# Key and query copies on ScalarE, constants and first weights at other places

## The chip, the cores and the metric

The kernel runs on one core of one Trainium2 chip. Its time is the device time of one execution in microseconds (us). The engines are named as the profile names them: PE (TensorE), ACT (ScalarE), DVE (VectorE), POOL (GpSimd) and SP (SyncE, which issues most of the DMA transfers). Each engine works through its own queue of instructions in order, and waits on semaphores for what the others must have done.

## The reference

A decoder trunk of two layers on one sequence of 512 tokens of width 1024, in float32. A layer is

```python
f = _swiglu(_rmsnorm(h, ffn1_pre_g[l]), ffn1_w_gate[l], ffn1_w_up[l], ffn1_w_down[l])
h = h + 0.5 * _rmsnorm(f, ffn1_post_g[l])
```

then a mixing step, then a second half-step of the first form. The mixing step projects the normalized h to queries, keys and values and adds three branches, each through its own output matrix and a sigmoid gate, before a common matrix `w_out`:

- stick-breaking attention, 8 heads of 64 channels, where the weight of a key is a sigmoid times the products of what later keys leave over;
- forgetting attention ("fox"), 8 heads of 64, a softmax whose logits get `c[q] - c[k]`, with `c` the running sum of the logarithms of forget gates;
- attention to a memory of 256 rows, 4 heads of 128.

## The kernel before

All matrix products are done in three passes. `split` writes a float32 value as a rounded high part (ACT, line 189 or 192) and the rest as a low part (DVE, line 190 or 193), and `mm3` adds high by high, high by low and low by high (lines 203 to 205). So each weight block of 128x1024 costs ACT one cast (`wh_...`), DVE one subtraction (`wl_...`) and PE its matmuls. Names are made of a letter for the tile, the layer, and numbers; the profile leaves the numbers out.

A layer runs as four stages: network a (gate and up products, tiles `pta`, in groups of hidden blocks `TG`, then down products), mixing (projections, heads, branch products `pb`), the product with `w_out` (`pwo`), and network c (`ptc`). The gate and up products go by a scheme of sums of weight blocks (`kta`, `ktc`) and of input blocks (`aga`, `ra`).

Heads go in pairs. A key projection `pk` (128 rows, 64 for each head) is split by halves into `k`: the high part of head j stands in `k[r, j]` with its own 64 rows `r`, and the other 64 rows `ro` of that tile are filled with a copy (lines 1544 and 1546), since the matmul contracts over 128 rows, high and low queries stacked. For the stick heads (branch 0) the low part is copied as well, in one instruction on two planes. The scores are `zs` (line 1317) or `zf` (1359 to 1367). A fox head adds a second matmul on `qk` (1367), a tile that `fox_pre` puts together from a copy of the queries, a copy of the low keys (1347, 1348), ones, and the running sums `cs` times a selector. `forget_cumsum` makes `cs`, with two copies (1462). The probabilities are then transposed and split (`pts`, `ptf`), multiplied with the values (`pvs`, `pvf`) and summed and split to `o`.

The PSUM bank of `pk` is read by ACT (high) and by DVE (low), and the build puts each reader of one tile behind the last one where they are on different engines.

What is issued when: the kernel text writes its work through a job queue `Q`. A job has weight units that are loaded ahead and a generator of products; `Q.add` appends, `Q.weave` and `Q.spawn` put generators with waits between the products, and `Q.past(mark, us)` holds a head until so much product time lies behind its projection (`W_K` is 4.0). `down` is used for the down products and for `w_out` alike: its job `first` loads the second half's weights, and with them the first two units of the next network (`marks["next"][0]`); its job `second` loads the first half's weights again, one unit behind each step. After that the build sorts the instructions of every engine by its own planning, so the place in the text is a wish and not the place in the queue. The places named below are those of the built queues.

Of the kernel before, what the change touches and what calls it, by code (L numbers as in the profile page):

```python
# [9 lines left out]
F32 = mybir.dt.float32  # L10
# [12 lines left out]
def kernel(  # L23
# [47 lines left out]
    NH = 8  # L71
# [637 lines left out]
    def ffn(l, src, wg, wu, wd, dst, name, spare, aside=None):  # L709
# [335 lines left out]
        if name == "a0":  # L1045
            Q.add([], vectors)
            Q.add([], lambda: iter(mem_squares() or ()))
        for g in TG[1:]:
            todo = after if g == TG[1] and after is not None else turns(g)
            some(1 if todo is after else 2)  # L1050
            over, later[:] = later[1:], later[:1]
            behind()
            some(7)
            later[:] = over
# [24 lines left out]
    def down(w, ktiles, act, emit, name, dst, marks, before=None, carry=False):  # L1079

        PAIRS = ((0, 1), (2, 3))
        AFTER = {(0, 0): ((0, 1),), (0, 1): ((1, 1),), (1, 1): ((2, 1), (3, 1)), (2, 1): ((2, 0),), (2, 0): ((3, 0),)}
        banks = {}

        def seed(hf, ts):

            for t, b in AFTER.get((ts[0], hf), ()) if carry else ():
                parts = HALVES if halves(b, t) else (FULL,)
                banks[t, b] = [pbank("mm", f"p{name}_{b}_{t}_{i}") for i in range(len(parts))]
                for pt, c in zip(banks[t, b], parts):
                    nc.scalar.activation(pt[:, c], dst.fs[t][:, HF[b]][:, c], AF.Copy, scale=-1.0 if b else 1.0)

        def halves(hf, t):
            return t == NT - 1 and dst.g_pre is None and hf == 0  # L1100

        def tiles(uns, hf, ts, done=None):
            seeded = (ts[0], hf) in banks
            pts = [banks.pop((t, hf))[0] if seeded else pbank("mm", f"p{name}_{hf}_{t}") for t in ts]
            for un in uns:
                for k in range(un.nk):
                    kk = un.k0 + k
                    for t, pt in zip(ts, pts):
                        ah, al = act(kk, slice(t * P, (t + 1) * P))
                        mm3(pt[:], ah, al, un.h[:, k], un.l[:, k], kk == 0 and not seeded, kk == ktiles - 1, seeded)  # L1110
                        yield 3 * S * PE_US
                    if kk == 1:
                        seed(hf, ts)
                if done is not None:
                    done()
            for t, src in [(t, emit(t, hf, pt[:], seeded)) for t, pt in zip(ts, pts)]:
                dst.result(t, hf, src)

        def at_last(uns, hf, t):

            parts = [(c, pt) for c, pt in zip(HALVES, banks.pop((t, hf)))]
            for i, (c, pt) in enumerate(parts):
                for un in uns:
                    for k in range(un.nk):
                        kk = un.k0 + k
                        ah, al = act(kk, slice(t * P, (t + 1) * P))
                        mm3(pt[:, c], ah, al, un.h[:, k, c], un.l[:, k, c], False, kk == ktiles - 1, True)
                        yield 3 * S // 2 * PE_US
                dst.last_part(t, hf, c, pt[:, c], i)

        def late(uns, hf, t):
            if halves(hf, t):
                yield from at_last(uns, hf, t)
                return
            Q.hold = True
            ends = t == NT - 1 and not marks["next"][0]
            yield from tiles(uns, hf, (t,), (lambda: Q.load_next(1)) if ends else None)
            Q.spawn(dst.chain(t))
            if ends:
                Q.hold = False  # L1140

        uns = [[Unit(w, k, 2, hf * S, S, f"{name}_{i}_{k}") for k in range(0, ktiles, 2)] for i, hf in enumerate((0, 1, 0))]

        def first():
            for un in uns[1] + marks["next"][0]:
                un.load()
            if before is not None:
                before()
            dst.gains()
            yield from tiles(uns[0], 0, PAIRS[0])  # L1150

        def second():

            again = iter(uns[2])
            yield from tiles(uns[1], 1, PAIRS[1], lambda: next(again).load())

        Q.add(uns[0], first)
        marks["next"] = [], []
        marks["late"] = Q.add([], lambda: iter(()))
        for t in PAIRS[0]:  # L1160
            Q.add(uns[1] if t == 0 else [], lambda t=t: late(uns[1], 1, t))
        Q.add(marks["next"][0], second)
        for t in PAIRS[1]:
            marks["end"] = Q.add(uns[2] if t == 2 else marks["next"][1], lambda t=t: late(uns[2], 0, t))

# [176 lines left out]
    def fox_pre(q, k, j, hd, cs, name):  # L1342

        r, ro, _ = HEAD_ROWS[j]
        rs_ = slice(ro.start, min(ro.stop, 104))
        qk = stile([P, 2, S], "rs", "qk" + name)
        nc.gpsimd.tensor_copy(qk[r, 0], q[r, j])
        nc.gpsimd.tensor_copy(qk[r, 1], k[r, 2])
        nc.gpsimd.memset(qk[ro, 0].bitcast(F32), 1.0)
        nc.vector.tensor_scalar(qk[rs_, 1], cs[rs_].bitcast(F32), sel[rs_, hd:hd + 1], None, ALU.mult)  # L1350
        return qk
# [89 lines left out]
    def forget_cumsum(l, fl, holder):  # L1441

        pt = pbank("mm", f"pfl{l}")
        for t in range(NT):
            nc.tensor.transpose(pt[:NH, t * P:(t + 1) * P], fl[:, t], ident[:])
        yield 0.3
        a, b = tmp(f"fa{l}")[:NH], tmp(f"fb{l}")[:NH]  # L1450

        nc.scalar.activation(a, pt[:NH], AF.Abs, bias=bfor[:, l:l + 1])
        nc.scalar.activation(a, a, AF.Exp, scale=-1.0)
        nc.scalar.activation(a, a, AF.Ln, bias=one_t[:NH])
        nc.vector.scalar_tensor_tensor(a, pt[:NH], nbfor[:, l:l + 1], a, ALU.min, ALU.subtract)
        nc.vector.tensor_tensor_scan(b, bfor[:, l:l + 1].broadcast_to([NH, S]), a, 0.0, ALU.add, ALU.add)
        cs = stile([P, S], "cs", f"cs{l}")
        nc.gpsimd.memset(cs[:].bitcast(F32), 0.0)
        nc.scalar.copy(cs[0:NH], b)
        nc.vector.tensor_tensor(cs[32:32 + NH], b, cs[0:NH].bitcast(F32), ALU.subtract)  # L1460
        for c in (0, 32):
            nc.gpsimd.tensor_copy(cs[64 + c:64 + c + NH], cs[c:c + NH])
        holder["cs"] = cs

    def mixing(l, src, ks, vs, values, dst):
# [62 lines left out]
        def proj(key, un, scale):  # L1528
            nm = f"{key[0]}{l}_{key[1]}_{key[2]}"
            pt = pbank("mm", "p" + nm)  # L1530
            yield from gemm(pt[:], [un], 0, act)
            if key[0] == "q":

                t = st[key] = blk("q", nm)
                for r, ro, j in HEAD_ROWS:
                    split(t[r, j], t[ro, j], pt[r], scale=scale)
            else:

                twice = key[1] == 0
                t = st[key] = stile([P, 4 if twice else 3, S], "k", nm)  # L1540
                for r, ro, j in HEAD_ROWS:
                    split(t[r, j], t[r, 2 + j if twice else 2], pt[r])
                    if twice:
                        nc.gpsimd.tensor_copy(t[ro, j::2], t[r, j::2])
                    else:
                        nc.gpsimd.tensor_copy(t[ro, j], t[r, j])

        def project_v(br, p):

# [206 lines left out]
        def run():  # L1756
# [47 lines left out]
            def causal(n):  # L1804

                if n % 2 == 0:
                    Q.past(marks[heads[n // 2]], W_K, Q.limit)
                if n == NH:
                    Q.until(marks["mem"])
                    st["o", 1] = [blk("o", f"o{l}_1_{p}") for p in range(NP)]  # L1810
# [123 lines left out]
    for l in LAYERS:  # L1934
        i, mn = 3 * l, []
        ma = ffn(l, subs[i], ffn1_w_gate, ffn1_w_up, ffn1_w_down, subs[i + 1], f"a{l}", "v",
                 lambda l=l, mn=mn: mem_norm(l, mn))
        values = mem_kv(l, mn, *kvs[l])
        mb = mixing(l, subs[i + 1], *kvs[l], values, subs[i + 2])
        if l == 0:  # L1940
            Q.weave(begin(), ma["first"])
            more_constants()
        else:
            for part, units in zip(mc["next"], (ma["early"][:2], ma["early"][2:])):
                part.extend(units)
            boundary(mc, mc["end"], ma["first"])
        boundary(ma, ma["end"], mb["first"])
        mb["run"]()
        mc = ffn(l, subs[i + 2], ffn2_w_gate, ffn2_w_up, ffn2_w_down, subs[i + 3], f"c{l}", "o")
        for part, units in zip(mb["next"], (mc["early"][:2], mc["early"][2:])):  # L1950
                part.extend(units)
        boundary(mb, mb["end"], mc["first"])
# [25 lines left out]
```

## Time and profile before

| what | value |
|---|---|
| median of 3 runs | 2342.62 us (2340.15 to 2343.8) |
| the profiled execution: its own time, its span | 2341.6 us, 2339.8 us |
| PE busy | 2326.2 us, 99% |
| DVE busy | 1815.4 us, 78% |
| ACT busy | 1429.4 us, 61% |
| POOL busy | 246.6 us, 11%, 330 instructions |
| granted clock | 0.999 |

A time such as 811.07 is counted from the start of the span. The second layer's mixing runs as the first one's, some 1158 us later. A row of a timeline has start, duration, engine, line, operation and shapes, and in brackets how long the engine stood idle before it and what ended that.

### The profile page before, as it was taken

Reading aid. Unit: us, or ns where it says so; the run is one execution under the profiler, and the core shown is the slowest. Engines: PE = TensorE matmul, PEld = TensorE weight load, DVE = VectorE, ACT = ScalarE, POOL = GpSimd, SP = SyncE. Lnnn points to the kernel's source line nnn. Section 1 sums busy time; section 2 is a strip of 40 time slices with the busy share of each in tenths; the row PEclk is TensorE's granted clock in tenths of the full one; section 3 lists DMA queues with packets and bytes.
Section 4 is the critical chain, followed back from the end, with each engine's and each line's share of the span. In section 5 each row is a group of like instructions: output and inputs, shape, how many; then the busy total and the mean of one; then the engine's idle time right before and its main releaser. Section 6 shows DMA issues by size and latency. Waiting matters only on the chain.

```text
span 2339.8 us, 32552 instructions
## 1 busy us (share of the span) xinstructions
PE 2326.2 (99%) x12232; PEld 1994.8 (85%) x12232; DVE 1815.4 (78%) x2407; ACT 1429.4 (61%) x2307; POOL 246.6 (11%) x330
## 2 busy tenths in 40 slices
PE   9999999999999999999999999999999999999998
PEld 8888889998888888888888888889988888888887
DVE  8766978676898887769887679786768988866696
ACT  6655766665665465567665567656656655556574
POOL 1101100100122011101011110011001210111110
PEclk9999999999999999999999999999999999999999
DMA  8866858753232676669586767587423326776682
GB/s 247 236 174 181 228 179 249 199 163 108 73 110 72 234 218 182 167 167 256 171 217 170 185 190 228 190 238 227 135 76 91 100 83 232 219 189 169 180 224 99
DMA packets 241697, 412.74 MB, mean 176 GB/s; under 512 B 12650, under 2 KB 78466, under 8 KB 241028
## 3 DMA queue, kind: packets, MB, share of 16 engines
q1 hardware_dynamic: 200992, 326.74, 42.5%
q0 software_dynamic: 37088, 71.34, 17.7%
q10 hardware_dynamic: 3460, 12.59, 1.4%
q8 instruction: 96, 1.57, 0.3%
q14 instruction: 61, 0.50, 0.1%
HBM read 383.35 MB, written 27.26 MB: 175 GB/s over the span
## 4 chain that ended last, share of the span: by engine, by line
PE 90%; DVE 5%; DMA 3%; ACT 1%; issue 1%; SPq 0%; POOL 0%; DVEq 0%; ACTq 0%; POOLq 0%
PE ptc L203 5%; PE ptc L205 5%; PE ptc L204 5%; PE pta L203 5%; PE pta L205 5%; PE pta L204 5%; PE g L203 3%; PE g L204 3%; PE g L205 3%; PE pdc L203 3%; PE pda L205 3%; PE pdc L205 3%; PE pdc L204 3%; PE pda L204 3%; PE pda L203 3%; PE pv L203 1%
## 5 line engine op out<-in xcount | busy, mean ns | idle before, releaser
L190 DVE TENSOR_TENSOR wl_tc<-ktc,wh_tc 128x1024 fp32r<-128x1024 f32 x80 | 97.7, 1223 | 63.3 <-ACT wh_tc L189 63.3
L190 DVE TENSOR_TENSOR wl_ta<-kta,wh_ta 128x1024 fp32r<-128x1024 f32 x80 | 97.6, 1223 | 57.8 <-ACT wh_ta L189 57.8
L205 PE MATMUL pta<-wh_ta,aga 128*128 128x512 f32 x320 | 124.7, 390 | 1.3 <-DVE aga L190 1.3
L189 ACT CAST wh_tc<-ktc 128x1024 fp32r<-128x1024 f32 x80 | 84.1, 1054 | 67.9 <-PE ptc L205 48.0
L203 PE MATMUL pta<-wh_ta,aga 128*128 128x512 f32 x320 | 125.2, 392 | 0.0
L203 PE MATMUL ptc<-wh_tc,agc 128*128 128x512 f32 x320 | 125.1, 393 | 0.0
L205 PE MATMUL ptc<-wh_tc,agc 128*128 128x512 f32 x320 | 124.6, 389 | 0.0
L204 PE MATMUL ptc<-wl_tc,agc 128*128 128x512 f32 x320 | 124.6, 389 | 0.0
L204 PE MATMUL pta<-wl_ta,aga 128*128 128x512 f32 x320 | 124.6, 389 | 0.0
L189 ACT CAST wh_ta<-kta 128x1024 fp32r<-128x1024 f32 x80 | 84.1, 1053 | 65.7 <-PE pta L205 41.8
L190 DVE TENSOR_TENSOR wl_tc<-raw_tc,wh_tc 128x1024 fp32r<-128x1024 f32 x56 | 68.6, 1224 | 45.4 <-ACT wh_tc L189 45.3
L190 DVE TENSOR_TENSOR wl_ta<-raw_ta,wh_ta 128x1024 fp32r<-128x1024 f32 x58 | 70.9, 1224 | 41.9 <-ACT wh_ta L189 41.8
L189 ACT CAST wh_ta<-raw_ta 128x1024 fp32r<-128x1024 f32 x58 | 60.9, 1052 | 45.5 <-PE pta L205 38.0
L189 ACT CAST wh_tc<-raw_tc 128x1024 fp32r<-128x1024 f32 x56 | 59.0, 1054 | 47.8 <-PE ptc L205 36.6
L203 PE MATMUL ptc<-wh_tc,us_b 128*128 128x512 f32 x224 | 87.7, 391 | 0.2
L203 PE MATMUL pda<-wh_da,aa 128*128 128x512 f32 x224 | 87.5, 391 | 0.0
L203 PE MATMUL pdc<-wh_dc,ac 128*128 128x512 f32 x224 | 87.5, 391 | 0.0
L205 PE MATMUL ptc<-wh_tc,us_b 128*128 128x512 f32 x224 | 87.2, 389 | 0.0
L204 PE MATMUL ptc<-wl_tc,us_b 128*128 128x512 f32 x224 | 87.2, 389 | 0.0
L205 PE MATMUL pda<-wh_da,aa 128*128 128x512 f32 x224 | 87.2, 389 | 0.0
L204 PE MATMUL pda<-wl_da,aa 128*128 128x512 f32 x224 | 87.2, 389 | 0.0
L204 PE MATMUL pdc<-wl_dc,ac 128*128 128x512 f32 x224 | 87.2, 389 | 0.0
(593 smaller groups left out, 7932.7 us busy)
## 6 DMA issues: line engine op xcount, KB each, us to landing
raw_ta<-in_ffn_w_gate_dram SPq DMA_DIRECT2D x44, 512.0 KB, 4.4
raw_tc<-in_ffn_w_gate_dram SPq DMA_DIRECT2D x44, 512.0 KB, 4.7
raw_da<-in_ffn_w_down_dram SPq DMA_DIRECT2D x42, 512.0 KB, 3.8
raw_dc<-in_ffn_w_down_dram SPq DMA_DIRECT2D x42, 512.0 KB, 3.6
kta<-in_ffn_w_up_dram SPq DMA_DIRECT2D x40, 512.0 KB, 6.2
raw_wg<-in_w_gate_dram SPq DMA_DIRECT2D x40, 512.0 KB, 4.7
ktc<-in_ffn_w_up_dram SPq DMA_DIRECT2D x40, 512.0 KB, 5.7
kt<-in_w_gate_dram SPq DMA_DIRECT2D x24, 512.0 KB, 5.9
```

The source lines that it names most:

```text
L189: both = [nc.scalar.copy(h_ap, src)]
L190: make = lambda: nc.vector.tensor_tensor(l_ap, src, h_ap.bitcast(F32), ALU.subtract)
L203: nc.tensor.matmul(pt, lh, rh, start=start, stop=False, skip_group_check=free)
L204: nc.tensor.matmul(pt, lh, rl, start=False, stop=False, skip_group_check=free)
L205: nc.tensor.matmul(pt, ll, rh, start=False, stop=stop, skip_group_check=free)
```

## The change

1. The copies of keys, queries and `cs` that POOL made are made by ACT. The copy of the keys' high part reads the PSUM bank `pk` in place of the tile `k`, and the one instruction for high and low planes of a stick head becomes two.
2. `more_constants`, which was called before everything else of layer 0 but the start, becomes a job ahead of the third group of hidden blocks of the first network.
3. In `down` without `carry` (that is, in the product with `w_out`) the first units of the next network are loaded in `second`, behind its third and fourth unit, and not in `first`.
4. `W_K` is raised by 1.5 for the first fox head. The built queues are the same on all engines with and without this edit.

```diff
+            if g == TG[2] and name == "a0":
+                Q.add([], lambda: iter(more_constants() or ()))
...
         def first():
-            for un in uns[1] + marks["next"][0]:
+            for un in uns[1] + (marks["next"][0] if carry else []):
                 un.load()
...
             again = iter(uns[2])
-            yield from tiles(uns[1], 1, PAIRS[1], lambda: next(again).load())
+            ahead = itertools.chain((None, None), () if carry else marks["next"][0], itertools.repeat(None))
+
+            def load():
+                for un in (next(again), next(ahead)):
+                    if un is not None:
+                        un.load()
+
+            yield from tiles(uns[1], 1, PAIRS[1], load)
...
-        Q.add(marks["next"][0], second)
+        Q.add(marks["next"][0] if carry else [], second)
...
-        nc.gpsimd.tensor_copy(qk[r, 0], q[r, j])
-        nc.gpsimd.tensor_copy(qk[r, 1], k[r, 2])
+        nc.scalar.copy(qk[r, 0], q[r, j].bitcast(F32))
+        nc.scalar.copy(qk[r, 1], k[r, 2].bitcast(F32))
...
-            nc.gpsimd.tensor_copy(cs[64 + c:64 + c + NH], cs[c:c + NH])
+            nc.scalar.copy(cs[64 + c:64 + c + NH], cs[c:c + NH].bitcast(F32))
...
                     split(t[r, j], t[r, 2 + j if twice else 2], pt[r])
+                    nc.scalar.copy(t[ro, j], pt[r])
                     if twice:
-                        nc.gpsimd.tensor_copy(t[ro, j::2], t[r, j::2])
-                    else:
-                        nc.gpsimd.tensor_copy(t[ro, j], t[r, j])
+                        nc.scalar.copy(t[ro, 2 + j], t[r, 2 + j].bitcast(F32))
...
-                    Q.past(marks[heads[n // 2]], W_K, Q.limit)
+                    Q.past(marks[heads[n // 2]], W_K + (1.5 if n == NH else 0.0), Q.limit)
...
-            more_constants()
```

The lines move: in the changed kernel the key copies are 1552 and 1554, `qk` 1356 and 1357, `cs` 1471, `zs` 1326, `zf<-qk` 1376.

ACT at the product with `w_out` of layer 0, first two tiles, before (`wh_wo` is the high part of a block of `w_out`, `w_tc` of the next network's first weights, `sqb` sums squares of `pwo`):

```order
L189 CAST wh_wo_1_4_7834<-raw_wo_1_4_7776 128x1024
L623 ACTIVATE sqb_0_0_7930,nfb_0_7872<-pwo_0_0_7880 128x512
L189 CAST w_tc_0_0_0_7846<-raw_tc_0_0_0_7826 128x1024
L189 CAST wh_wo_1_6_7840<-raw_wo_1_6_7816 128x1024
L189 CAST w_tc_0_0_2_7851<-raw_tc_0_0_2_7832 128x1024
L623 ACTIVATE sqb_1_0_7933,nfb_1_7873<-pwo_0_1_7881 128x512
```

and where the `w_tc` rows stand in the changed kernel, one stage later (`us_b` is the next network's input):

```order
L189 CAST wh_wo_2_6_7952<-raw_wo_2_6_7852 128x1024
L623 ACTIVATE sqb_3_1_8119,nfb_3_7873<-pwo_1_3_8022 128x512
L189 CAST w_tc_0_0_0_8078<-raw_tc_0_0_0_7950 128x1024
L192 ACTIVATE us_b_0_8089<-utb_1_0_8132 128x4x128
L189 CAST w_tc_0_0_2_8111<-raw_tc_0_0_2_7956 128x1024
L192 ACTIVATE us_b_1_8090<-utb_1_1_8139 128x4x128
```

The two casts left the first pass over `w_out` and stand among those of the second token tile's input; `wh_wo_1_6` follows `sqb` directly now.

ACT at the third stick pair (`k_0_2`), before:

```order
L189 CAST k_0_2_5749<-pk_0_2_5676 64x512
L189 CAST o_0_1_4615<-ss_1_0_5735 64x512
L189 CAST k_0_2_5749<-pk_0_2_5676 64x512
L189 CAST pts_1_1_5795<-pts_1_1_0_5797 128x512
L189 CAST pts_1_1_5795<-pts_1_1_1_5804 128x384
L189 CAST pts_1_1_5795<-pts_1_1_2_5810 128x256
```

and in the changed kernel:

```order
L189 CAST k_0_2_5753<-pk_0_2_5680 64x512
L189 CAST o_0_1_4615<-ss_1_0_5739 64x512
L1552 CAST k_0_2_5753<-pk_0_2_5680 64x512
L1554 CAST k_0_2_5753<-k_0_2_5753 64x512
L189 CAST k_0_2_5753<-pk_0_2_5680 64x512
L189 CAST pts_1_1_5801<-pts_1_1_0_5803 128x512
L1552 CAST k_0_2_5753<-pk_0_2_5680 64x512
L1554 CAST k_0_2_5753<-k_0_2_5753 64x512
L189 CAST pts_1_1_5801<-pts_1_1_1_5810 128x384
L189 CAST wh_v_1_2_3_5768<-raw_v_1_2_3_5618 128x792
L189 CAST pts_1_1_5801<-pts_1_1_2_5816 128x256
```

Four copies stand between the casts, two of them ahead of the second cast of `pts`, and the cast of a value weight has come ahead of the third. PE's queue at this place has changed too: `zs_2_0`, `pvs_1_1` and the first rows of `pq_0_3`, which stood one behind the other, are interleaved.

ACT at the first fox heads, from the weight cast on, before:

```order
L192 ACTIVATE wh_wb_0_0_0_6440<-raw_wb_0_0_0_6273 128x1024
L189 CAST k_1_2_6433<-pk_1_2_6384 64x512 x2
L189 CAST wh_q_1_0_6541<-raw_q_1_0_6382 128x1024
L1371 ACTIVATE pf_2_0_3_6497,stf_2_0_6485<-zf_2_0_3_6489,stf_2_0_6485 128x512
L1371 ACTIVATE pf_2_0_2_6504,stf_2_0_6485<-zf_2_0_2_6488,stf_2_0_6485 128x384
```

and in the changed kernel:

```order
L192 ACTIVATE wh_wb_0_0_0_6448<-raw_wb_0_0_0_6281 128x1024
L189 CAST k_1_2_6441<-pk_1_2_6392 64x512
L1552 CAST k_1_2_6441<-pk_1_2_6392 64x512
L189 CAST k_1_2_6441<-pk_1_2_6392 64x512
L1357 CAST qk_2_0_6488<-k_1_2_6441 64x512
L1552 CAST k_1_2_6441<-pk_1_2_6392 64x512
L1357 CAST qk_2_1_6530<-k_1_2_6441 64x512
L189 CAST wh_q_1_0_6549<-raw_q_1_0_6390 128x1024
```

Four copies that were POOL's stand in ACT's queue here, and four more (two of `cs`, two of `qk` from the queries) ahead of the weight cast.

## The prediction

> **What bounds the kernel now.** I read the page first: the busy shares, then the chain that ended last.
>
> ```profile
> PE 2326.2 (99%) x12232; PEld 1994.8 (85%) x12232; DVE 1815.4 (78%) x2407; ACT 1429.4 (61%) x2307; POOL 246.6 (11%) x330
> PE 90%; DVE 5%; DMA 3%; ACT 1%; issue 1%; SPq 0%; POOL 0%; DVEq 0%; ACTq 0%; POOLq 0%
> ```
>
> TensorE (PE) works 99% of the span and POOL is 0% of the chain. The change removes no matmul, so all it can win is idle time of PE. The waits of PE say how much there is (us in total, times, longest):
>
> ```profile
> PE pwo L204 <- DVE wl_wo L190: 1.6, 2, 0.9
> PE zf L1367 <- POOL qk L1348: 1.4, 2, 1.0
> PE pta L205 <- DVE aga L190: 1.3, 1, 1.3
> PE zf L1359 <- DVE ptf L190: 0.5, 2, 0.2
> ```
>
> These are the waits that the change can touch: 4.8 us. Read by start to start (a 512-column fp32r matmul follows the last one after 0.23 us, see the two `pwo` rows below) each costs a little more, because PE starts late and its pipeline has run empty. So the ceiling of any gain is near 5.5 us, 0.23% of 2341.6. Below I call a difference under 0.2% (4.7 us) no change; that is about what a measurement of this kernel can tell. What remains is what the change adds to ScalarE (ACT), a queue served in order, and whether PE waits for that.
>
> **Part 1, w_out: the next network's first weights move away.**
>
> ```profile
> 807.56 1.05 ACT L189 CAST w_tc<-raw_tc 128x1024 fp32r<-128x1024 f32 x1 [1.78 <-DMA raw_tc<-in_ffn_w_gate_dram]
> 808.52 1.04 ACT L189 CAST wh_wo<-raw_wo 128x1024 fp32r<-128x1024 f32 x1
> 809.79 1.22 DVE L190 TENSOR_TENSOR wl_wo<-raw_wo,wh_wo 128x1024 fp32r<-128x1024 f32 x1
> 809.68 0.44 PE L203 MATMUL pwo<-wh_wo,ms 128*128 128x512 f32 x1
> 811.07 0.50 PE L204 MATMUL pwo<-wl_wo,ms 128*128 128x512 f32 x1 [0.95 <-DVE wl_wo L190]
> ```
>
> ACT stands 1.78 us at `w_tc` for a transfer; `wh_wo` is queued behind it, `wl_wo` behind that on VectorE (DVE), and PE starts 1.39 us after the row before instead of 0.23: 1.16 us lost. In layer 1 the same wait is shorter (1.6 in total less 0.95 is 0.66), about 0.82 start to start. With the two `w_tc` rows gone, ACT is free some 1.5 us earlier and DVE has 1.2 us less ahead, so both waits go: **−2.0 us**. Both ends: 0 if `raw_wo` itself lands late, −2.0.
>
> Where they go: their two transfers are issued behind the save of h, their casts stand between those of the second tile's `us_b`.
>
> ```profile
> raw_tc<-in_ffn_w_gate_dram SPq DMA_DIRECT2D x6, 512.0 KB, 4.2
> 834.64 1.28 DVE L193 SCALAR_TENSOR_TENSOR us_b<-utb,us_b 128x512 fp32r<-128x512 f32 x2
> 841.30 0.39 PE L203 MATMUL ptc<-w_tc,us_b 128*128 128x512 f32 x1
> ```
>
> On DVE two 1.2 us subtractions come ahead of `us_b`, which moves its end from 835.92 to about 838.8 with the wait for ACT; PE wants it at 841.3 less the 1.2 us won, 840.1. So 1.3 us of cover are left, against a landing of 4.2 us after issue. I take 0; gone, it costs what the transfer is later than 1.3 us.
>
> **Part 2, start: the constants go behind the second group.** On DVE they stand between 28.5 and 35.8, on POOL two selections are among them.
>
> ```profile
> 28.51 0.17 DVE L144 MEMSET c<- 128x128 f32 x1
> ...
> 35.63 0.17 DVE L159 COPY sel<-c 104x8 f32<-104x8 f32 x1
> ...
> 44.81 1.06 ACT L1174 ACTIVATE mst<-mst 128x1024 f32<-128x1024 f32 x1 [3.99 <-DMA mst<-in_mem_dram]
> 59.48 2.35 DVE L190 TENSOR_TENSOR aga<-ra,aga 128x1024 fp32r<-128x1024 f32 x2
> 59.05 0.39 PE L204 MATMUL pta<-wl_ta,aga 128*128 128x512 f32 x1
> 60.76 0.50 PE L205 MATMUL pta<-wh_ta,aga 128*128 128x512 f32 x1 [1.31 <-DVE aga L190]
> 69.93 1.23 DVE L190 TENSOR_TENSOR wl_ta<-raw_ta,wh_ta 128x1024 fp32r<-128x1024 f32 x1
> 121.87 1.22 DVE L190 TENSOR_TENSOR wl_ta<-kta,wh_ta 128x1024 fp32r<-128x1024 f32 x1
> ```
>
> The constants' time on DVE, by their rows some 2.6 us, does not come out at the other end: ACT still waits for `mst` until 44.81, and `hida` and `aga_3` hang behind it. What is won is one 1.1 us row (a `kta` subtraction) that now runs in DVE's idle time before 46, so `aga` begins at 58.4 and PE waits 0.4 instead of 1.5: −1.1. But the new order has PE take four instead of two matmuls of the group's `wh_ta_4_0_0` early, and DVE has four small `mem_rstd` rows and one `wl_ta` more before its `wl_ta_4_0_0` (69.93 before, about 71.6 now) where PE arrives at about 70.8: +0.8. Net **−0.3 us**, between −1.5 and +0.8. At their new place they stand around the `wl_ta` at 121.87, which PE takes up at about 130, so some 7 us cover their 2.6: nothing.
>
> **Part 3, the copies.** All of POOL's copies go to ACT, which has 98 instructions more, 49 a layer. Two of POOL's groups:
>
> ```profile
> L1544 POOL CAST k<-k 64x1024 fp32r<-64x1024 f32 x16 | 17.3, 1080 | 80.1 <-DVE k L190 49.0 <-issue 31.1
> L1348 POOL CAST qk<-k 64x512 fp32r<-64x512 f32 x16 | 11.9, 743 | 11.4 <-DVE k L190 11.0
> 672.15 0.58 ACT L189 CAST k<-pk 64x512 fp32r<-64x512 f32 x1 [3.40 <-DVE k L190]
> ```
>
> By the last row an ACT copy of 64x512 is 0.58 us; a 64x1024 copy becomes two. 98 × 0.58 is 57 us of ACT, whose idle share is 39%: room in sum, but a queue in order is decided place by place. Two things are worse than on POOL. The copy of the high half now reads PSUM behind DVE's low part of the same half (the built order has it wait there), so ACT stands until DVE is through; POOL could copy at once. And ACT's next casts are queued behind it.
>
> *Fox switch* (first forgetting heads):
>
> ```profile
> 671.44 0.68 DVE L190 TENSOR_TENSOR k<-pk,k 64x512 fp32r<-64x512 f32 x1
> 672.18 0.61 POOL L1348 CAST qk<-k 64x512 fp32r<-64x512 f32 x1 [2.76 <-DVE k L190]
> 672.00 0.48 PE L1366 MATMUL zf<-k,q 128*128 128x512 f32 x1
> 672.85 0.50 PE L1367 MATMUL zf<-qk 104*128 104x512 f32 x1 [0.38 <-POOL qk L1348]
> ```
>
> Today only one POOL copy lies between DVE's `k` (ends 672.12) and PE. After, three ACT copies do: the one that `zf<-k,q` needs, then the other half's high part, then `qk`. DVE itself may come 0.3 us earlier (below): 671.83, copy to 672.45, high part to 672.95, `qk` to 673.5. PE starts `zf<-qk` 0.65 later than 672.85; 1.0 later if DVE gains nothing. I take 0.8 in each layer: **+1.6 us** (ends: −1.9 if both waits vanish, +2.4).
>
> *Third stick pair* (heads at 612 and again at 1771): PE is here only 0.3 us behind DVE, and ACT's casts of `pts` come in between.
>
> ```profile
> 609.28 0.58 ACT L189 CAST k<-pk 64x512 fp32r<-64x512 f32 x1 [0.87 <-DVE k L190]
> 610.40 1.42 ACT L189 CAST pts<-pts 128x512 fp32r<-128x512 f32 x4 [0.54 <-PE pts L1302]
> 610.47 0.69 DVE L190 TENSOR_TENSOR k<-pk,k 64x512 fp32r<-64x512 f32 x1
> 611.20 1.68 DVE L190 TENSOR_TENSOR pts<-pts,pts 128x512 fp32r<-128x512 f32 x4
> 612.25 1.45 PE L1317 MATMUL zs<-k,q 128*128 128x512 f32 x8
> ```
>
> After, at 609.28 ACT does two copies first, so the second high part ends at 610.9 instead of 609.86 and DVE's second low at 611.6. Only then may ACT's third copy start (`L1552` ahead of the second `pts` cast): 611.6 to 612.2, fourth to 612.7, `pts` cast to 613.2, DVE's part of it to 613.75. The `zs` matmuls of 384 columns take over that bank; PE wants them at 612.95: 0.8 us of wait, and about 0.2 more at the 256-column ones, which stand behind ACT's first sigmoids. **+2.0 us** for both layers (ends 0 and +3.2). At the fourth pair the same count leaves 0.25 us to spare, at the second 1.2: nothing.
>
> *Second fox pair*, where DVE is held up by POOL:
>
> ```profile
> 692.54 1.09 DVE L190 TENSOR_TENSOR o<-sf,o 64x512 fp32r<-64x512 f32 x1
> L190 DVE TENSOR_TENSOR o<-sf,o 64x512 fp32r<-64x512 f32 x16 | 12.6, 788 | 2.9 <-ACT o L189 2.7
> L190 DVE TENSOR_TENSOR o<-ss,o 64x512 fp32r<-64x512 f32 x16 | 10.9, 684 | 2.9 <-ACT o L189 2.7
> 663.80 0.98 DVE L1460 TENSOR_TENSOR cs<-fb,cs 8x512 fp32r<-8x512 f32 x1
> ```
>
> The same subtraction takes 684 ns in the stick heads and 1.09 us where a POOL copy runs beside it. Without POOL the chain to `ptf` is 0.4 us earlier; of the 0.5 us in the list about 0.2 a layer is won, since `qk` now comes late by ACT: **−0.4 us** (ends −0.5 and +0.3). [...]
>
> The edit of W_K by 1.5 for the ninth head changes no row of the built order: 0.
>
> **Sum.** −2.0 − 0.3 + 1.6 + 2.0 − 0.4 = +0.9 us on the profiled execution's 2341.6, so 2342.5. The median of the runs shown, 2342.62, is 1.0 above that execution: **2343.5 us**, no change.
>
> **The rivals.**
>
> *All of PE's waits go* and none comes: −2.0 − 1.5 − 1.9 − 0.5, 5.9 at the most, 2337 us. For it: ACT is idle 39%. Against: at the fox switch ACT's copies are in series behind DVE by the built order. Were the two switch waits merely unchanged, it would be −4 and within 0.2%. Chance 0.10, of which 0.07 beyond 0.2%.
>
> *ACT sets the pace of the heads* (slower). The place is the second key copy of each pair, ahead of casts which PE needs. If ACT's rows come just 0.3 us later than I count (0.61 for each copy and a wake-up behind each of its waits for DVE), the fourth stick pair loses its 0.25 us and then the 1.0 of the third, and the third and fourth fox pairs some 0.5: 2 × (1.0 + 1.0) more, with the fox switch at its upper end (+0.8): about +5.7 us, 2348 to 2349. From 0.25 us on it decides. For it: every stick `k` wait of ACT above doubles. Against: the cover elsewhere is over 1 us. Chance 0.14.
>
> *The moved weights are late*: `w_tc` lands over 1.3 us later than its median, the first `ptc` waits. Then part 1 gives back 1 to 2 us: 2345, inside no change. Chance 0.06.
>
> **How the numbers follow.** Forecast 0.70, around 2343.5, its own range 2341 to 2346. With the others: faster by over 0.2% (below 2338) 0.07, the same 0.79, slower (above 2347.3) 0.14. The range reaches to both: 2339.5 to 2348.
>
> **What would show it.** Right: `pwo <- wl_wo` gone from PE's waits; `zf L1376 <- ACT qk` at about 1.0 to 1.8 a layer in place of POOL's; a new wait of `zs` at the third stick pair near 612; ACT busy up by some 55 us, POOL down by about the same. Wrong: no `zs` wait (then about 2341.5), or `zs` and `zf` waits at most pairs (then the slower rival).

## The result, and the profile after

| kernel | median | runs | profiled execution: its own time, its span |
|---|---|---|---|
| before | 2342.14 us | 6 | 2341.6, 2339.8 |
| changed | 2350.78 us (2349.47 to 2352.48) | 6 | 2352.48, 2350.6 |

The ratio is 1.0037, with a 95% interval of 1.0025 to 1.005: slower by 8.6 us, where no change was forecast (2343.5, range 2339.5 to 2348). The changed kernel's two profiled executions have 2352.48, which is the slowest of these six, and, in the last experiment, 2349.81 us. So the profile read below holds 10.8 us of loss, 2.2 more than the medians show.

The page of the changed kernel, busy time of each engine:

```profile
PE 2332.0 (99%) x12232; PEld 1997.0 (85%) x12232; DVE 1814.1 (77%) x2407; ACT 1481.7 (63%) x2391; POOL 191.5 (8%) x262
```

ACT gained 52 us of work and 84 instructions (the prediction spoke of 98; one copy for each of 42 places a layer is what ran), POOL lost 55 us. PE is busy 6 us longer with the same 12232 matmuls; about half of that is no matter of waits and comes below. The waits of PE (us in total, times, longest):

```profile
PE zs L1326 <- DVE pts L190: 3.5, 4, 1.1
PE zf L1375 <- ACT k L1552: 2.6, 2, 1.6
PE zf L1376 <- issue: 1.6, 2, 0.8
PE zf L1376 <- ACT qk L1357: 0.8, 2, 0.4
```

The `pwo` wait for `wl_wo` and the `pta` wait for `aga` have gone from the list. In their place stand 3.5 us at the third stick pair and 5.0 us at the fox heads. The signs by which the prediction was to be known for right are all there, the `zf` waits larger than it said (2.1 us a layer without the second fox pair, against 1.0 to 1.8); they tell where PE waits, and not what that costs.

Where the time went is read best by laying the two profiled executions' matmuls side by side, the same matmul in each, and noting by how much it starts later in the changed kernel. The difference stays constant over hundreds of microseconds and moves in steps; the larger ones are these:

| place (time before) | predicted, a layer | layer 0 | layer 1 |
|---|---|---|---|
| start, 60 to 78 | -0.3 once | -0.9 | |
| third stick pair, 612 and 1771 | +1.0 | -0.85 to +1.64: +2.5 | 5.16 to 7.62: +2.5 |
| fox switch, 672 and 1830 | +0.8 | 1.80 to 3.44: +1.6 | 7.79 to 9.44: +1.65 |
| the 3.4 us behind it | 0 | 3.44 to 4.98: +1.5 | 9.44 to 10.95: +1.5 |
| second fox pair, 697 and 1856 | -0.2 | 4.98 by 4.71 to 5.32: +0.3 | 10.95 by 10.68 to 11.25: +0.3 |
| `pb<-o`, 781 and 1940 | 0 | +1.2 | +0.4 |
| w_out, 811 and 1964 to 1970 | -1.2, -0.8 | 6.45 to 5.16: -1.3 | 12.05 to 10.42: -1.6 |

They add up to 9.7; the last matmul is 10.8 later, as is the span. The rest are steps of 0.15 to 0.4, among them the fourth stick pair (+0.15 in each layer), and, in layer 1, the fourth fox pair (+0.4) and `pwo` at 1994 (+0.4). The `pb<-o` row of layer 0 is a transfer that landed 6.3 us after its issue here and 5.1 before, and no part of the change. Of layer 1's -1.6 at w_out, 0.7 lies at 1964, a wait for `ms` that the second profile of the changed kernel has again (0.8).

**Third stick pair.** The changed kernel's rows, ACT and DVE, then PE (start, duration, and in brackets the idle time before it and what ended it):

```profile
609.45 0.58 ACT L1552 CAST k<-pk 64x512 fp32r<-64x512 f32 x1 [0.87 <-DVE k L190]
609.93 0.62 ACT L1554 CAST k<-k 64x512 fp32r<-64x512 f32 x1
610.57 0.58 ACT L189 CAST k<-pk 64x512 fp32r<-64x512 f32 x1
...
611.91 0.58 ACT L1552 CAST k<-pk 64x512 fp32r<-64x512 f32 x1
612.51 0.62 ACT L1554 CAST k<-k 64x512 fp32r<-64x512 f32 x1
613.15 0.48 ACT L189 CAST pts<-pts 128x384 fp32r<-128x384 f32 x1
...
611.19 0.69 DVE L190 TENSOR_TENSOR k<-pk,k 64x512 fp32r<-64x512 f32 x1 [0.58 <-ACT k L189]
611.91 0.69 DVE L190 TENSOR_TENSOR pts<-pts,pts 128x512 fp32r<-128x512 f32 x1
613.66 0.56 DVE L190 TENSOR_TENSOR pts<-pts,pts 128x384 fp32r<-128x384 f32 x1 [1.06 <-ACT pts L189]
...
612.66 0.72 PE L1326 MATMUL zs<-k,q 128*128 128x512 f32 x2 [1.09 <-DVE pts L190]
614.28 0.62 PE L1326 MATMUL zs<-k,q 128*128 128x384 f32 x2 [0.66 <-DVE pts L190]
```

The second wait, 0.66, is the one that was predicted, with its chain: the copies at 611.91 and 612.51, the cast of `pts` at 613.15, DVE at 613.66, PE at 614.28. The first, 1.09, was not: DVE's part of the 512-column `pts` starts 0.71 later than before (611.20), and PE is here 0.85 earlier. Of the 0.71, some 0.5 come of this pair's own first two copies, which stand ahead of the second high part (DVE waits 0.58 for it); the prediction had 0.4 of that in its chain. The other 0.17, and that ACT and DVE have not come 0.85 earlier as PE has, is 1.0 us of lateness that was made one pair ahead. ACT's first sigmoid of the second pair, before:

```profile
588.51 0.60 ACT L1323 ACTIVATE as<-zs 128x512 f32<-128x512 f32 x1 [1.92 <-PE zs L1317]
```

and in the changed kernel, with two of its four copies:

```profile
587.63 0.58 ACT L1552 CAST k<-pk 64x512 fp32r<-64x512 f32 x1 [0.76 <-DVE k L190]
588.23 0.62 ACT L1554 CAST k<-k 64x512 fp32r<-64x512 f32 x1
588.87 0.60 ACT L1332 ACTIVATE as<-zs 128x512 f32<-128x512 f32 x1
```

Before, ACT stood idle for 1.92 us until PE had made `zs`; now it comes from the copies, 0.36 later than before, where PE is 0.85 earlier. PE does not wait there, its cover is large enough. But from here to the third pair ACT and DVE hang on each other, not on PE, and make up only 0.2 of the 1.2 us: the third pair's `o` cast on ACT (607.96) is still 0.17 later than before, 1.0 us further behind PE, before that pair's copies begin. With the stick copies on POOL (an experiment below) PE, ACT and DVE all run 0.23 us ahead of their old times through both pairs. No run moves the second pair's copies alone, so how much of the third pair's wait is owed to them is read from these rows and not tested by itself.

**Fox switch.** ACT, DVE and PE of the changed kernel:

```profile
671.41 1.06 ACT L192 ACTIVATE wh_wb<-raw_wb 128x1024 fp32r<-128x1024 f32 x1
...
674.36 0.58 ACT L1552 CAST k<-pk 64x512 fp32r<-64x512 f32 x1 [1.42 <-DVE k L190]
674.96 0.58 ACT L189 CAST k<-pk 64x512 fp32r<-64x512 f32 x1
675.57 0.62 ACT L1357 CAST qk<-k 64x512 fp32r<-64x512 f32 x1
...
668.05 0.69 DVE L190 TENSOR_TENSOR pts<-pts,pts 128x512 fp32r<-128x512 f32 x1 [0.56 <-ACT pts L189]
...
672.50 1.23 DVE L193 SCALAR_TENSOR_TENSOR wl_wb<-raw_wb,wh_wb 128x1024 fp32r<-128x1024 f32 x1 [0.25 <-ACT wh_wb L192]
673.65 0.68 DVE L190 TENSOR_TENSOR k<-pk,k 64x512 fp32r<-64x512 f32 x1
...
674.99 0.50 PE L1375 MATMUL zf<-k,q 128*128 128x512 f32 x1 [1.01 <-ACT k L1552]
676.28 0.47 PE L1376 MATMUL zf<-qk 104*128 104x512 f32 x1 [0.79 <-issue]
```

ACT's `wh_wb` is 4.2 us later than before (667.23) where PE is 1.8 later: the two copies of `cs` and two of `qk` stand ahead of it, 4 x 0.62 = 2.5. DVE comes out of `cs` 0.3 earlier, as predicted, but then it waits twice for ACT: 0.56 for the cast of `pts`, which stands behind the two copies of `cs`, and 0.25 for `wh_wb`. So `k` is 2.2 later than before, 0.4 more than PE. Then the three copies in series: 0.60 from start to start, not 0.5.

**What PE does behind the switch.** Each row is a stretch of the changed kernel: its bounds, its length, PE busy, the TensorE clock that was granted (1.00 is full), the DMA share, GB/s.

```profile
677.50:677.56 0.06, 0.06 (x2) 0.82 0.00 0
678.00:680.00 2.00, 2.00 (x8) 0.50 0.83 231
680.90:680.96 0.06, 0.06 (x1) 0.57 0.00 0
...
1841.44:1841.50 0.06, 0.06 (x1) 0.87 1.12 341
```

For 3.4 us behind each switch the granted clock is half, and 512-column matmuls follow each other after 427 ns instead of 227. In the first row 0.82 is 0.038 us at full and 0.022 at half, so the half begins at 677.54, and by the third it ends at 680.95. This is 3.0 us of the loss in this execution and about half of PE's longer busy time; 1.5 of the rest lie at the two third stick pairs, where the rows of matmuls behind a wait are longer (0.72 us for two). Nothing in the prediction spoke of the clock.

### The profile page after: what moved, and what is told of

It reads as the page before. It is cut to its first block, busy times and chain, and to the rows that moved or that the text cites. A ratio compares the mean times of both kernels' runs of the same rounds, so it can differ in the third digit from the quotient of the medians.

```text
span 2350.6 us, 32579 instructions
## 1 busy us (share of the span) xinstructions
PE 2332.0 (99%) x12232; PEld 1997.0 (85%) x12232; DVE 1814.1 (77%) x2407; ACT 1481.7 (63%) x2391; POOL 191.5 (8%) x262
## 4 chain that ended last, share of the span: by engine, by line
PE 93%; DVE 3%; ACT 2%; issue 1%; DMA 1%; DVEq 0%; ACTq 0%; SPq 0%
PE ptc L203 5%; PE ptc L205 5%; PE ptc L204 5%; PE pta L203 5%; PE pta L204 5%; PE pta L205 5%; PE g L203 3%; PE g L204 3%; PE g L205 3%; PE pdc L205 3%; PE pda L205 3%; PE pdc L204 3%; PE pdc L203 3%; PE pda L203 3%; PE pda L204 3%; PE pv L204 1%
## 5 line engine op out<-in xcount | busy, mean ns | idle before, releaser
L203 PE MATMUL pdc<-wh_dc,ac 128*128 128x512 f32 x224 | 87.5, 391 | 0.0
L205 PE MATMUL pdc<-wh_dc,ac 128*128 128x512 f32 x224 | 87.2, 389 | 0.0
```

The source lines that it names most:

```text
L203: nc.tensor.matmul(pt, lh, rh, start=start, stop=False, skip_group_check=free)
L205: nc.tensor.matmul(pt, ll, rh, start=False, stop=stop, skip_group_check=free)
```

## The experiments

The kernel before ran beside each group, at 2341.0 to 2341.4 us.

### The parts apart

**moves_only**: the constants and the weights as in the change, all copies on POOL as before.

```diff
-        nc.scalar.copy(qk[r, 0], q[r, j].bitcast(F32))
+        nc.gpsimd.tensor_copy(qk[r, 0], q[r, j])
...
-                    nc.scalar.copy(t[ro, j], pt[r])
...
+                        nc.gpsimd.tensor_copy(t[ro, j::2], t[r, j::2])
```

> The change without its copies: the copies stay on POOL, the constants and the first weights are moved. By the two traces the start gained 0.98 us and the passes over w_out 1.4 and 0.7 us, start to start. Theory of two places (the loss sits where PE waits for the copies): 2342.1 - 3.0, about 2339. Rival, the moves themselves cost something (a transfer or an order that collides): 2342 or more. Waits of PE: zf <- POOL qk back at about 1.4 us, no zs wait, no pwo wait.

Measured 2338.38 us, ratio 0.9989 (0.998 to 0.9998). Of the waits at the heads there is left, above 0.5 us:

```profile
PE zf L1376 <- POOL qk L1357: 1.1, 2, 0.6
```

**copies_only**: the copies on ACT, constants and weights at their old places (`more_constants()` called where it was, `marks["next"][0]` in `first`).

> The copies alone on ScalarE, constants and first weights where they were before. Theory of two places: the whole loss and the old waits at the start and at w_out as well, 2350.8 + 3.0, about 2353.5. Rival, the moves cost: about 2350 or less.

Measured 2354.05 us, ratio 1.0057 (1.0044 to 1.0069). So the copies are the whole loss, +13.0 us, and the rest of the change is a gain of 2.6. The two add up to 10.4, where the change as a whole was measured at 8.6.

**constants_only** and **weights_only**: one of the two moves each, copies on POOL.

> Of the change, the move of the attention constants behind the second group alone (copies on POOL, next network's weights at their old places). Theory, from the trace of the kernel with both moves: the 1.3 us wait of pta for aga near 60 goes (1.48 start to start) and one of about 0.4 us for wl_ta near 70 comes, net -1.1 us: about 2340.1 where before is 2341.2; the pwo waits for wl_wo (1.6 in the list) stay. Rival, the prediction's term of -0.3: a wait of 0.8 for wl_ta, 2340.9. The two times lie within what the measurement tells apart; the start-to-start rows decide.

> Of the change, the next network's first weights in the middle products alone (copies on POOL, constants at their old place). Theory: both pwo waits for wl_wo go (1.16 and 0.82 start to start), the first ptc products are not late, the 1.3 us wait of pta for aga stays: 2341.2 - 2.0 = 2339.2. Rival (the weights' own wait takes the place): a wait of ptc for w_tc near 840 of 1 us or more, then 2340.2 or above.

Measured 2340.0 us, ratio 0.9995 (0.9986 to 1.0004), and 2339.24 us, ratio 0.999 (0.9981 to 0.9999). The wait that each leaves, of the first and then of the second:

```profile
PE pwo L204 <- DVE wl_wo L190: 1.4, 2, 0.8
```

```profile
PE pta L205 <- DVE aga L190: 1.2, 1, 1.2
```

Each move takes away its own wait and leaves the other. The weights are worth 2.2 us (2.0 predicted), and no `ptc` wait for `w_tc` comes. The constants' 1.4 us lie within what the times tell apart from nothing; by the start-to-start rows the wait of 1.48 for `aga` goes and 0.4 comes at 70.7.

### Which copies

**stick_on_pool**: the stick heads' key copies back on POOL, those of the fox heads on ACT. **fox_on_pool**: the reverse.

```diff
                     if twice:
-                        nc.scalar.copy(t[ro, 2 + j], t[r, 2 + j].bitcast(F32))
+                        nc.gpsimd.tensor_copy(t[ro, j::2], t[r, j::2])
+                    else:
+                        nc.scalar.copy(t[ro, j], pt[r])
```

> The changed kernel, but the 32 key copies of the stick heads stay on POOL; those of the fox heads are on ScalarE. Theory of two places: the waits at the third stick pair (2.1 us a layer start to start, and some 0.4 us of slower matmuls) go, those at the fox switch stay: 2350.8 - 5, about 2346. Rival, each copy costs the same wherever it stands (a spread loss of 11 us over 84 copies): 32 of 84 of 11.6, about 2346.5, so the time alone does not tell these two apart, the list of waits does: by the two places no zs wait is left and the zf waits are as they were; by the spread one both become smaller.

> The changed kernel, but all copies of the fox heads (keys, qk, cs: 52 of the 84) stay on POOL; those of the stick heads are on ScalarE. Theory of two places: the zs waits of the third stick pair stay (2.5 us a layer), the fox switch is as before the change (0.6 and 1.2 us), and no stretch of half clock is left: 2339 + 5, about 2344. Rival, spread: 2350.8 - 52/84 of 11.6, about 2343.6; by it the zs waits shrink as well.

Measured 2346.93 us, ratio 1.0027 (1.0016 to 1.0038), and 2344.08 us, ratio 1.0013 (1.0005 to 1.0022). Waits of the first:

```profile
PE zf L1375 <- ACT k L1555: 2.9, 2, 1.5
PE zf L1376 <- issue: 1.6, 2, 0.8
```

and of the second:

```profile
PE zs L1326 <- DVE pts L190: 3.5, 4, 1.1
PE zf L1376 <- POOL qk L1357: 0.4, 1, 0.4
```

The waits at the two places don't depend on each other: with either set of copies back on POOL its waits go and the other's stay to 0.3 us. So the loss is not spread evenly over the copies. Against moves_only the stick copies cost 5.7 us and the fox copies 8.6. That is 14.3 in sum, where all copies cost 13.0 in copies_only, and the change is 12.4 above moves_only (11.3 when each is set against the kernel before that ran beside it): the sizes are good to a microsecond or two only, and the seven runs with the stick copies on POOL lie between 2344.9 and 2350.7.

### Why ACT comes late

**copy_from_high**: the copy of the high part reads the tile `k` in SBUF, as POOL's did, in place of the PSUM bank. In the built queue it no longer stands behind DVE's read of that bank.

```diff
-                    nc.scalar.copy(t[ro, j], pt[r])
+                    nc.scalar.copy(t[ro, j], t[r, j].bitcast(F32))
```

> The changed kernel, but ScalarE's copy of the keys' high part reads the high part in SBUF that it has just written, not the PSUM bank, so it needn't stand behind VectorE's low part. Theory (the fox switch is one chain in series, ScalarE behind VectorE): zf <- ACT k gone (1.2 and 1.8 us start to start), the wait for qk stays and grows to about 1.5, since the other half's high part still stands behind VectorE; at the third stick pair nothing is won (2 us a layer: the pts casts stand behind all four copies now). In all 1.4 us less, and up to 3 us more where a stretch of half clock goes with it: 2346.5 to 2349.5. Rival, the PSUM read is not what delays: 2350.8.

Measured 2344.64 us, ratio 1.0017 (1.0008 to 1.0025): 6.1 us less than the change (5.2 when each is set against the kernel before that ran beside it), and below what was expected.

```profile
PE zf L1376 <- issue: 3.1, 2, 1.5
PE zs L1326 <- DVE pts L190: 1.7, 2, 0.9
PE zf L1375 <- ACT k L1552: 0.3, 1, 0.3
```

At the third stick pair ACT's copy of the second high part starts with DVE's low part, both at 609.39, and not behind it (611.19 and 611.91 in the changed kernel). The `zf` wait for `k` is nearly gone, and the one for `qk`, which still needs DVE's low part, has grown from 0.8 to 1.5 a layer; both were expected. What was not is that the third stick pair wins: the second of its two `zs` waits is gone. The first stays (0.9), but not for the reason that it has in the changed kernel. The lateness from the pair ahead has gone: up to this pair's copies PE, ACT and DVE all run 1.14 us ahead of their old times. Now all four copies of this pair stand ahead of the casts of `pts`, for which DVE waits:

```profile
610.77 1.42 ACT L189 CAST pts<-pts 128x512 fp32r<-128x512 f32 x4
611.39 1.68 DVE L190 TENSOR_TENSOR pts<-pts,pts 128x512 fp32r<-128x512 f32 x4 [1.30 <-ACT pts L189]
```

That ACT's copy stood in its queue behind DVE is thus a good half of the stick pairs' loss, 2.5 to about 1.1 us a layer; by these rows the rest is the time that the copies themselves take on ACT. ACT and DVE hold each other up: the groups of the changed kernel's `k` (instructions, busy us, mean ns, then the idle time before them and what ended it),

```profile
L190 DVE TENSOR_TENSOR k<-pk,k 64x512 fp32r<-64x512 f32 x32 | 21.9, 686 | 13.7 <-ACT k L189 13.5
L1552 ACT CAST k<-pk 64x512 fp32r<-64x512 f32 x32 | 18.6, 582 | 26.3 <-DVE k L190 25.4
```

ACT's copy waits for DVE's low part, and DVE's next low part for ACT's next high part, which is queued behind the copy. Before, DVE's idle time at these rows was 3.5 us.

**change_and_later_fox** and **moves_and_later_fox**: the first fox head's products are asked for 2 us later, in the change and in moves_only.

```diff
-                        Q.spawn(causal(n + 1), W_NEXT)
+                        Q.spawn(causal(n + 1), W_NEXT + (2.0 if n + 1 == NH else 0.0))
```

> The whole change, and the first fox head spawned 2 us later in the plan as in the run beside it: 1.9 us of other work ahead of the fox scores. Theory: of the 2.2 and 2.9 us of waits at the switch some 1.9 a layer are covered, and the half clock goes with them: 2350.8 - 3.8 to - 6.5, 2344 to 2347; the zs waits of the third stick pair stay as they are. Rival (the copies push the chain back by as much as is put ahead): 2350 or more.

> The moves without the copies, and the first fox head spawned 2 us later in the plan, by which the built queue puts the last stick head's value product (8 matmuls) and three matmuls of a projection ahead of the fox scores, 1.9 us of work. Theory: the fox switch waits for a fixed chain on VectorE, so work ahead of it covers the wait: the zf <- POOL qk waits (0.70 and 0.87 us start to start in moves_only) go, 2338.4 - 1.6, about 2337. Rival, the chain is pushed back with the queue (VectorE has the sums of that value product to do as well): 2338 or more.

Measured 2346.71 us, ratio 1.0025 (1.0015 to 1.0036), and 2338.95 us, ratio 0.9991 (0.9983 to 1.0). Waits of the first, then of the second:

```profile
PE pvf L1298 <- ACT ptf L189: 1.6, 2, 0.8
PE zf L1376 <- ACT qk L1357: 1.3, 3, 0.5
```

```profile
PE pvf L1298 <- ACT ptf L189: 0.9, 2, 0.4
PE pq L203 <- DVE k L190: 0.6, 2, 0.3
```

In the change a later place wins 3 to 4 us, the lower end of what was expected: PE no longer idles for `k`, no half clock is left in that profile, and the `zs` waits stay (3.4 us). Without the copies on ACT it wins nothing. POOL's `qk` wait goes, but two others of the same size come, `pvf` and `pq`: by the waits the rival of that run was right, while the times of the two (2337, and 2338 or more) lie too close together to tell.

### The half clock

**filled_wait**: 20 more matmuls with the causal mask ahead of the first fox head's products, so that PE works through the first of the two waits at the switch.

```diff
+        for _ in range(20 if hd_first else 0):
+            nc.tensor.matmul(pzs[NT - 1][:, (NT - 1) * P:], ident16, causal16[:], start=False, stop=False,
+                             skip_group_check=True)
```

> The changed kernel with the causal mask added 20 more times to one bank ahead of the first fox head's first product, in each layer, so that TensorE works for some 1.1 us of the time in which it waits for ScalarE's copy of the keys (masked logits get -2e31 instead of -1e30, the rest is the same). Theory, the half clock comes of idle time piling up: the wait for the copy falls from 1.0 and 1.6 us to 0 and 0.5, no half clock is left behind the switch (678 to 681 and 1842 to 1845 in the changed kernel's profile), and the time falls by up to 3 us to 2348 though the heads begin no earlier. Rival, the half clock has nothing to do with the waits: it stays, and the time stays at 2350.8 or rises.

Measured 2351.74 us, ratio 1.0043 (1.0029 to 1.0056), of 5 runs that lie between 2349.2 and 2353.3. The time does not fall to 2348. The clock, behind the switch and in layer 1 behind the third stick pair:

```profile
678.00:680.00 2.00, 2.00 (x12) 1.00 0.91 256
1781.00:1783.00 2.00, 2.00 (x9) 0.50 0.74 258
```

The half clock at both switches has gone, though PE waits for `qk` as before: with the first wait filled, the second alone (0.8 us) is not followed by one. But one has come behind a pair of `zs` waits, which had none in the changed kernel, and PE lost another 1.5 us at a `g` product near 1580 that waits for `qm`. So the theory of that run had the clock behind the switch right and the time wrong, and the half clock is not a matter of the switch alone.

**change_again**: the changed kernel as it is, profiled once more, to test what decides.

> The changed kernel as it is, profiled once more. In the profile so far PE ran 512-column matmuls every 427 ns instead of 227 in two stretches, 677.55 to 680.97 and 1841.49 to 1844.91: both 3.42 us long, and 1163.94 us apart, which is 341 times 3.4133 us. Theory: the clock is set anew at the end of each window of 3.413 us, and the windows run on whatever the kernel does; a window in which PE idles for 1.9 us or more is followed by one at half clock, one with 1.7 us or less is not. Each half window costs about 1.6 us. In this execution the windows lie elsewhere: with the ends of whatever half stretches it has, each other half stretch ends a whole number of 3.413 us away (to 0.1 us), every window with at least 1.9 us of idle in the four clusters of waits (near 612, 674, 1776, 1839: 2.1, 2.2, 2.1 and 2.9 us) is followed by a half one, and none with 1.7 or less. Rival: the half clock follows a wait by its length alone, so that it comes again exactly behind the two fox switches and not behind the two stick pairs, at distances that are no multiple of 3.413. Time: 2350.8 by both, with runs some 1.6 us apart by the number of half windows.

Measured 2349.81 us (2349.13 to 2350.68), ratio 1.0037 (1.0024 to 1.0049). PE at the two switches:

```profile
674.68 0.50 PE L1375 MATMUL zf<-k,q 128*128 128x512 f32 x1 [1.10 <-ACT k L1552]
675.97 0.47 PE L1376 MATMUL zf<-qk 104*128 104x512 f32 x1 [0.79 <-issue]
...
1836.24 0.49 PE L1375 MATMUL zf<-k,q 128*128 128x512 f32 x1 [1.13 <-ACT k L1552]
1837.54 0.47 PE L1376 MATMUL zf<-qk 104*128 104x512 f32 x1 [0.80 <-issue]
```

and the clock behind each:

```profile
678.00:680.00 2.00, 2.00 (x12) 1.00 0.83 252
...
1838.20:1838.30 0.10, 0.10 (x2) 0.57 0.49 143
1839.00:1841.00 2.00, 2.00 (x9) 0.50 0.75 204
```

The same two waits, equal to 0.03 us, and the clock halves behind one only. Their length alone does not decide, and the rival is out. The place in a fixed raster does. In the first profile of the changed kernel the two half stretches are 3.41 us long each (677.54 to 680.95, 1841.48 to 1844.90). They begin 1163.94 us apart, and the clock falls once more behind the last matmul, at 2346.66, 505.18 us after the second: both distances are whole multiples of one length, 341.0 and 148.0 x 3.4133 us. In change_again the half begins at 1838.214; 341 x 3.4133 earlier is 674.27, in the middle of the first switch's first wait, so its idle time falls in two windows, 0.84 and 1.5 us. At the second switch both waits lie in the window 1834.80 to 1838.21. In the executions other than that first profile one edge, of its half stretch or of the fall behind the last matmul, gives the raster, which is taken to run through the whole execution as its edges show it there. The idle time of PE in each window behind the start, counted as all time beyond the usual step between its matmuls:

| execution | window | idle in it | clock in the next |
|---|---|---|---|
| changed | 1838.07 to 1841.48 | 2.86 | half |
| change_again | 1834.80 to 1838.21 | 2.44 | half |
| copy_from_high | 1831.54 to 1834.96 | 2.34 | half |
| copies_only | 612.52 to 615.93 | 2.27 | half |
| stick_on_pool | 1830.73 to 1834.14 | 2.26 | half |
| changed | 674.12 to 677.54 | 2.02 | half |
| filled_wait | 1776.75 to 1780.16 | 2.01 | half |
| copies_only | 1776.46 to 1779.88 | 2.00 | full |
| fox_on_pool | 610.59 to 614.00 | 1.97 | full |
| change_and_later_fox | 1772.21 to 1775.63 | 1.93 | full |
| copy_from_high | 671.01 to 674.42 | 1.89 | full |
| change_and_later_fox | 611.69 to 615.11 | 1.88 | full |

All other windows have 1.73 or less, and full clock behind them. So the theory holds, but not with the 1.9 that it was given: three windows above that were followed by full clock. These windows put the bound near 2.0 us, found after the fact. The idle times are good to some 0.03 us, so 2.00 and 2.01 don't tell it more finely. About 2.0 of the 3.41 us were enough here, put together from two waits.

## Why the prediction was wrong, step by step

- **Part 1, w_out, -2.0.** Right: the waits went where it was said, -2.2 us in the run with the weights alone. The moved weights' own cover held. (The step of 0.23 us is not in the two rows that the prediction points at, 809.68 and 811.07, which span the wait; the `pwo` rows ahead of them, 809.45 and 809.68, have it.)
- **Part 2, start, -0.3.** The mechanism was right, the new wait was too large: 0.4 us for `wl_ta` in the run with the constants alone (0.6 in the change) in place of 0.8. The net is -0.9 in the traces.
- **Part 3, third stick pair, +2.0 for both layers; measured +5.0.** The chain behind the second copy came as predicted, 0.66 us of PE's wait. What failed is the sentence on the second pair, "1.2: nothing". No wait of PE followed there, but ACT came out of it 1.2 us later against PE, the chain of ACT and DVE made up only 0.2 of it, and the third pair began 1.0 us further behind PE. With the shift of the second high part, which was worked out but not followed to the first bank, that gives the 1.09 there, and the sum had nothing for it.
- **Fox switch, +1.6; measured +3.3.** The chain of three copies was right. Two sizes were off: DVE was to come 0.3 earlier and came 0.4 later than PE, because ACT's four copies ahead of `wh_wb` made DVE wait for `pts` (0.56) and for `wh_wb` (0.25), waits that the working did not look for though it had these copies in ACT's queue; and a copy in series costs 0.60 from start to start, not 0.5.
- **The half clock, not foreseen: +3.0 in this profile,** 1.5 for each window; the second profile of the changed kernel has one such window. The sum took a wait's price to be its own length.
- **Second fox pair, -0.4; measured +0.6.** The gain came: DVE's `o<-sf` did fall, from 788 to 683 ns, and `cs` from 0.98 to 0.68, which is the 0.3 us that the fox switch had counted for DVE. PE begins the pair 0.27 us earlier in each layer, where 0.2 was counted. But that `qk` comes late by ACT was taken only as a bound on the gain and given no price of its own: PE waits 0.38 us for it at 703.01 and loses 0.6 from start to start.
- **The rivals.** "ACT sets the pace of the heads" came nearest, in its sign and in its size (2348 to 2349 against 2350.78), and its counter-argument, over 1 us of cover elsewhere, is the step that failed above. Its places were not right: the fourth stick pair lost 0.15 us a layer, the third fox pair nothing. "All of PE's waits go" and late weights did not happen.
- **The range** left no room for several places being mis-sized on the same side, which they were. At the third stick pair and at the fox switch the cause was one: ACT's lateness was costed anew at each place as though ACT came there on time. The half clock came on top.

moves_only beats both kernels: 2338.38 us, 0.11% below the kernel before, with its interval from 0.02 to 0.2%.

## What to carry to other kernels

Work added to an engine's queue was not free here where it was covered: ACT came out of the second stick pair 1.2 us later against PE, PE did not wait there, and 1.0 us of it was left at the third pair, some 20 us on. So add up the additions from the last place at which that engine, or the one that it feeds, stood idle, not from the wait in question. A copy that read a bank behind another engine held up its queue (25.4 us of ACT's idle time in all, ended by DVE's `k`), and reading the finished copy elsewhere won back about half of the loss here (2350.78 to 2344.64 us), with the copies still on ACT; putting them back on POOL won all of it (2338.38 us). Two short waits of TensorE close together (1.13 and 0.80 us in one window of 3.41 us) were followed by a half-clock stretch that cost 1.5 us on top; 0.8 us alone was not. Keep such waits apart, or fill one, though filling one took only the half clock away from its place here, and no time from the kernel (2351.74 us).

## What the runs showed of the hardware that was not expected

- The granted TensorE clock goes to half for one window of 3.41 us behind a window with 2.01 us of idle time or more, 7 of 7 such windows in thirteen executions; behind none with 2.00 or less did it. Where the windows lie against the waits changes from execution to execution: in one profile of the changed kernel a window began at 674.12 and held nearly all of the first switch's idle time (2.02 us), in the other an edge at 674.27 cut it in 0.84 and 1.5 us. So the same kernel loses 1.5 us at one place or not.
- A 64x512 copy on ACT takes 0.58 us by its row out of PSUM and 0.62 out of SBUF, and in a row of them each mostly follows the last after 0.60 to 0.65 us (0.48 at 609.45). POOL's took 0.71 to 0.78 on average by group, but stood in a queue with hardly anything else in it (POOL was busy 11% of the span before).
